# Padded constants, units pinned to source order, and wider openings in the gated merges of a hybrid decoder layer

## The chip, the cores and the metric

The kernel runs on one core of one Trainium2 chip. The metric is the device time in microseconds (us) of the whole program. The kernel before takes 2725.5 us (median of 3 runs, 2723.21 to 2727.9).

## What is computed

One decoder layer over 512 tokens of 2048 channels, in fp32. A modulated norm of x gives u; one wide input projection of u feeds three token mixers (A: differential attention, B: retention, C: dilated windows), their SiLU gates and three merge gates; the gated branches are merged and go through w_out.

```python
u = rms_norm(x, norm_w) * (1.0 + scale[:, None]) + shift[:, None]
proj = jnp.einsum('bsd,de->bse', u, w_in)
...
y_a = jnp.einsum('bsw,wd->bsd', o_a.astype(dt) * jax.nn.silu(a_z), w_proj_a)
y_b = jnp.einsum('bsw,wd->bsd', o_b.astype(dt) * jax.nn.silu(b_z), w_proj_b)
y_c = jnp.einsum('bsw,wd->bsd', o_c.astype(dt) * jax.nn.silu(c_z), w_proj_c)
merged = jax.nn.sigmoid(g_a) * y_a + jax.nn.sigmoid(g_b) * y_b + jax.nn.sigmoid(g_c) * y_c
y = jnp.einsum('bsd,de->bse', merged, w_out)
return x + gate[:, None] * y
```

## The kernel before, in words

**Precision.** Every operand of a matmul is kept as a high part (fp32r) and a low part (the rest). A product is three matmuls (`mm3`, L148 to L151): high by high, high by low, low by high. So each weight tile is loaded by SP, cast by ACT (the high part) and subtracted by DVE (the low part), in `w_half` (L144, L145), for the units in `pure_prep` (L549, L550) and `sum_prep` (L580 to L582).

**Stages**, in us from the start of the span:

- 0 to 244: modulation, norm, u, and the first merge-gate columns, as high and low products of u by weights.
- 244 to 974, the units: nine "units" of 1024 columns of w_in (five for values, four for merge gates of A and B) are made by a Strassen-like scheme with seven products instead of eight. A unit is 14 jobs. Six are plain (P1, P2, R3, two jobs each): load 1 MB, cast, low part, matmuls. Eight are sum jobs (j = 0 to 7): load, four sums in place (L580), cast (L581), low part (L582), matmuls into four results R6, R5, R7 and Q4. A job of a value unit is 24 matmuls of 512 columns, one of a gate unit (`fm=True`) 48 of 256. In a value unit the tokens are the stationary operand, in a gate unit the weights. The loop at L652 prepares job i + 1, then multiplies job i; in the first eight jobs `form_build` also makes the sums of tokens (the forms). When a group of products is complete its `done` runs: `keep`, `p2_done` or `sum_done`, with DVE sums, a sigmoid on ACT for gate units, and a write on POOL's queue.
- 974 to 1678, eight C heads; 1776 to 2092, eight A heads; 2212 to 2432, four pairs of B heads. Each is a row of projections (`proj`, two halves of 1024 rows, 48 matmuls of 512) with the attention work of the head put between the halves as `mid`.
- 1678 to 1776, 2092 to 2212 and 2432 to 2537, a gate phase after each (`gate_phase`, L692): 16 blocks db of 128 columns, 24 matmuls each; the result times the merge gate (L730), plus the part so far (L729 loads it into gpr, L732 adds), written back to part.
- 2537 to 2722: the product with w_out, residual and final norm.

**Memory.** Pools lie on the left or the right side of SBUF. The constants come first on the left; weights for the stages after the units, xr, xh and xl of the units, and mh and ml lie on the left; u (uh, ul), the forms (fh, fl) and the mixers' results (yh, yl) on the right. The weights of the first stage are on the right as well. `xr` has three buffers, `xh` and `xl` two each. PSUM has two tiles `pj` and six tiles `at`.

**What sets the order.** The framework schedules the instructions into one queue per engine, which then runs in order. It may put an instruction ahead of one that stands earlier in the source if it expects it to be ready sooner; source order is the priority. `tc.keep_in_program_order(ins)` ties `ins` behind the instruction that was traced before it on the same engine; it orders issue only and waits for nothing else. No instruction of the units is tied before the change.

**Gate phases.** `y_start` opens a block's product with six of eight slots of y, in an `at` tile, because the last two slots come late. Three blocks are opened ahead (`ahead`), with the leftovers of the last head (`left`) run between them; then each block is closed with j = 6 and 7.

**Bias of the C gates.** `gate_bias_load` (L671) loads and sums on POOL into br (one buffer), `gate_bias_sum` closes it with one matmul (L688). `bias_step` runs at each C head and a second time in head 1.

Of the kernel before, what the change touches and what calls it, by code (L numbers as in the profile page):

```python
# [17 lines left out]
P = 128  # L18
# [46 lines left out]
def hybrid_kernel(ctx, tc, x, c, w_in, w_pa, w_pb, w_pc, w_out, w_ada, b_ada, norm_w, lam,  # L65
# [49 lines left out]
    nlam = const.tile([P, 1], F32, tag="nlam", name="nlam")  # L115
    daw = const.tile([P, 1], F32, tag="daw", name="daw")

    uh = [up.tile([P, S], F32R, tag=f"uh{i}", name=f"uh{i}") for i in range(KC)]
    ul = [up.tile([P, S], F32R, tag=f"ul{i}", name=f"ul{i}") for i in range(KC)]

# [12 lines left out]
    def w_half(src, k0, c0, rot=False, tiles=None, low=dve):  # L133
# [11 lines left out]
            low.tensor_sub(l, r, h.bitcast(F32))  # L145
        return h, l

    def mm3(ps, ah, al, bh, bl, start, stop):  # L148
        nc.tensor.matmul(ps, lhsT=ah, rhs=bh, start=start, stop=False)  # L149
        nc.tensor.matmul(ps, lhsT=ah, rhs=bl, start=False, stop=False)  # L150
        nc.tensor.matmul(ps, lhsT=al, rhs=bh, start=False, stop=stop)  # L151
# [12 lines left out]

    def perm(ap):
# [335 lines left out]
    def form_build(j):  # L501

        if j % 2 == 0:
            r = wxp.tile([P, 4, 512], F32, tag="xr", name="xr", bufs=3)
            for i in range(2):
                nc.sync.dma_start(out=r[:, 2 * i:2 * i + 2, :],
                                  in_=u_dram[i * HJ + j:i * HJ + j + 2].rearrange("j p t -> p j t"))
            form_rows[0] = r
        r, jj = form_rows[0], j % 2
        d = evp.tile([P, 4, 256], F32, tag=("z", "s")[jj], name="d")  # L510
        a11, a21 = r[:, jj, 0:256], r[:, jj, 256:512]
        a12, a22 = r[:, 2 + jj, 0:256], r[:, 2 + jj, 256:512]
        dve.tensor_sub(d[:, 0, :], a21, a22)
        dve.tensor_sub(d[:, 1, :], a11, d[:, 0, :])
        dve.tensor_sub(d[:, 3, :], a21, a11)
        dve.tensor_sub(d[:, 2, :], a12, d[:, 1, :])
        act.copy(fh[j], d)
        dve.tensor_sub(fl[j], d, fh[j].bitcast(F32))

    def tokens(name, j, qs):  # L520

# [19 lines left out]
    def unit_jobs(w, c0, put, fm=False, early=False):  # L541
# [17 lines left out]
        def keep(key, tag):  # L559
            t = evp.tile([P, 2, 512], F32, tag=tag, name=tag)  # L560
            for q in range(2):
                act.copy(t[:, q, :], st[key][q])
            st[tag] = t

        def p2_done():
            t = evp.tile([P, 2, 512], F32, tag="c", name="c")
            for q in range(2):
                dve.tensor_add(t[:, q, :], st["p1"][:, q, :], st["P2"][q])
            put(t, 0, 0)
            if early:  # L570
                nc.gpsimd.dma_start(out=p1_dram, in_=st["p1"])

        def sum_prep(j):
            r, h, l = x_tiles()
            for i in range(2):
                nc.sync.dma_start(out=r[:, 2 * i:2 * i + 2, :],
                                  in_=w[(i * HJ + j) * P:(i * HJ + j + 1) * P, c0:c0 + 1024]
                                  .rearrange("p (a c) -> p a c", a=2))
            for o, a in ((0, 1), (1, 3), (3, 0), (2, 3)):
                dve.tensor_add(r[:, o, :], r[:, o, :], r[:, a, :])  # L580
            act.copy(h, r)  # L581
            dve.tensor_sub(l, r, h.bitcast(F32))  # L582
            return h, l

        def sum_mul(j, hl):
# [10 lines left out]
        def sum_done():  # L596
            z = evp.tile([P, 2, 512], F32, tag="z", name="z")
            s = evp.tile([P, 2, 512], F32, tag="s", name="s")
            r3, p1 = st["r3"], st["p1"]
            for q in range(2):  # L600
                dve.tensor_sub(z[:, q, :], st["R6"][q], p1[:, q, :])
            for q in range(2):
                dve.tensor_add(s[:, q, :], z[:, q, :], st["R5"][q])
            dve.tensor_add(r3, r3, s)
            put(r3, 0, 512)
            for q in range(2):
                dve.tensor_add(z[:, q, :], z[:, q, :], st["R7"][q])
                dve.tensor_add(s[:, q, :], s[:, q, :], st["R7"][q])
            put(s, 1, 512)
            for q in range(2):  # L610
                dve.tensor_sub(z[:, q, :], st["Q4"][q], z[:, q, :])
            put(z, 1, 0)

        lists = []
        for key, name, k0, cc, done in (("P1", "A11", 0, 0, lambda: keep("P1", "p1")),
                                        ("P2", "A12", 1024, 0, p2_done),
                                        ("R3", "2", 1024, 512, lambda: keep("R3", "r3"))):
            lists.append([(lambda k0=k0, cc=cc, t=t: pure_prep(k0 + t * 512, c0 + cc),
                           lambda hl, key=key, name=name, t=t: pure_mul(key, name, t, hl),
                           done if t == HJ // 4 - 1 else None) for t in range(HJ // 4)])  # L620
        lists.append([(lambda j=j: sum_prep(j), lambda hl, j=j: sum_mul(j, hl),
                       sum_done if j == HJ - 1 else None) for j in range(HJ)])
        return lists[0] + lists[1], lists[2] + lists[3]

    def put_values(unit):
# [21 lines left out]
    for n, b in enumerate([NF - 1] + list(range(NF - 1))):  # L647
        if n % 2 == 0:
            t = evp.tile([P, 2, 512], F32, tag=("p1", "c", "r3", "s")[n // 2], name="raw")
        (act.copy if n % 2 == 0 else dve.tensor_copy)(t[:, n % 2, :], ps[b])  # L650
        nc.scalar.dma_start(out=graw_dram[NF + NM + b], in_=t[:, n % 2, :])
    for i, (_, mul, done) in enumerate(jobs):  # L652
        nxt = jobs[i + 1][0]() if i + 1 < len(jobs) else None
        if i < HJ:
            form_build(i)
        mul(ready)
        ready = nxt
        if done is not None:
            done()
    wx_es.close()  # L660
    ev_es.close()
    fo_es.close()
# [23 lines left out]
    def gate_bias_sum(db, br):  # L686
        pc = at()
        nc.tensor.matmul(pc[:, 0:1], lhsT=br, rhs=ones[:, 0:1], start=True, stop=True)  # L688
# [250 lines left out]
    for hd in range(8):  # L939
# [187 lines left out]
    for pr in range(4):  # L1127
# [25 lines left out]
        szs = [silu(bp, proj(B_Z + (2 * pr + a) * P, mid=lambda a=a, rest=rest: rest(a)), tag=f"sz{a}", bufs=1)  # L1153
               for a in range(2)]

        def values(a, pr=pr, vpair=vpair, pts=pts, got=got):
# [126 lines left out]
```

## Time and profile before

| what | us |
|---|---|
| median of 3 runs | 2725.5 |
| the profiled execution | 2723.54 |
| its span | 2721.8 |
| first stage, 0 to 120 and 120 to 244: PE busy | 95.76 and 115.24 |
| C heads, 974 to 1678: PE busy of 704 | 693.01 |
| gate phase C, 1678 to 1776: PE busy of 98 | 95.35 |
| A heads, 1776 to 2092: PE busy of 316 | 314.31 |
| w_out, 2537 to 2722: PE busy of 185 | 176.51 |

The profile is of one execution. The engines are PE (matmuls), DVE (vector), ACT (scalar), POOL and SP (which issues most loads). In a group of instructions, a line reads: code line, engine, operation, output and inputs with shapes, count, then busy time and mean ns of one, then idle time of the engine just before them and what ended it. In a timeline, a row is start, duration, engine, line, and in brackets the idle time before it. A matmul's duration in the records overlaps the next one's, so the pace of PE is read from start to start. A line of the waits is: who waited, for whom, then us in total, number of waits, the longest.

### The profile page before, as it was taken

What the parts mean: (1) busy time and instruction counts of PE and PEld (TensorE: products, weight loads), DVE (VectorE), ACT (ScalarE), POOL (GpSimd) and SP (SyncE); (2) the same over time, 40 slices, a digit from 0 to 9 for tenths busy, and PEclk for the clock granted to TensorE, in tenths of its full rate; (3) what the DMA queues carried; (4) which work ended last, traced back from release to release, by engine and by line L of the source; (5) the groups of instructions that cost most, each with busy time, mean ns of one, the idle gap of its engine ahead of it and who ended that gap; (6) DMA issues with size and microseconds to landing.
All of it is one profiled execution on the core that took longest, in us unless ns stands there. A gap on an engine that the chain in (4) does not pass through costs nothing.

```text
span 2721.8 us, 33257 instructions
## 1 busy us (share of the span) xinstructions
PE 2608.9 (96%) x13091; PEld 2184.7 (80%) x13091; DVE 1698.1 (62%) x2455; ACT 1034.2 (38%) x1388; POOL 265.2 (10%) x271
## 2 busy tenths in 40 slices
PE   6899999999999999899999999999999899998998
PEld 5777777778999978688888888788887677777888
DVE  7985887777787744344443444657666667776434
ACT  4224433334343433333333333246665124443222
POOL 3331000000000022222211220000000000000000
PEclk9999999999999999999999999999999899999999
DMA  9777666666666654344443444942322672325632
GB/s 347 246 268 253 221 213 209 216 216 203 208 199 205 209 134 137 89 117 114 115 117 103 112 122 116 285 133 79 92 86 86 222 246 87 107 82 171 217 103 101
DMA packets 413420, 448.17 MB, mean 165 GB/s; under 512 B 24696, under 2 KB 308042, under 8 KB 412112
## 3 DMA queue, kind: packets, MB, share of 16 engines
q1 hardware_dynamic: 383784, 395.61, 46.0%
q0 software_dynamic: 9760, 33.59, 4.0%
q10 hardware_dynamic: 19720, 16.86, 1.8%
q8 instruction: 102, 1.67, 0.3%
q14 instruction: 54, 0.44, 0.1%
HBM read 405.56 MB, written 40.44 MB: 164 GB/s over the span
## 4 chain that ended last, share of the span: by engine, by line
PE 77%; DVE 12%; DMA 6%; ACT 2%; issue 2%; POOL 0%; SPq 0%; ACTq 0%; DVEq 0%; POOLq 0%
PE pj L151 15%; PE pj L149 14%; PE pj L150 14%; PE at L150 10%; PE at L151 10%; PE at L149 10%; DVE acc L309 3%; DMA xr<-in_w_in_dram 2%; DVE xl L550 1%; DMA part<-gsg 1%; DVE rs L992 1%; DVE rt L1102 1%; DVE wl L145 1%; ACT xh L549 1%; DMA gpr<-part 1%
## 5 line engine op out<-in xcount | busy, mean ns | idle before, releaser
L151 PE MATMUL pj<-uh,wl 128*128 128x512 f32 x1552 | 616.6, 397 | 11.2 <-DVE wl L145 8.7
L149 PE MATMUL pj<-uh,wh 128*128 128x512 f32 x1552 | 620.5, 400 | 4.8 <-ACT wh L144 4.8
L150 PE MATMUL pj<-ul,wh 128*128 128x512 f32 x1552 | 614.8, 396 | 0.0
L145 DVE TENSOR_TENSOR wl<-wr,wh 128x1024 fp32r<-128x1024 f32 x226 | 285.2, 1263 | 383.1 <-ACT wh L144 363.8
L144 ACT CAST wh<-wr 128x1024 fp32r<-128x1024 f32 x228 | 238.8, 1049 | 562.7 <-PE pj L150 411.3
L151 PEld LDWEIGHTS pj<-uh,wl 128*128 128x128 f32 x1552 | 293.5, 189 | 83.0 <-DVE wl L145 11.2
L149 PEld LDWEIGHTS pj<-uh,wh 128*128 128x128 f32 x1552 | 293.7, 189 | 69.8 <-ACT wh L144 5.0
L150 PEld LDWEIGHTS pj<-ul,wh 128*128 128x128 f32 x1552 | 294.0, 189 | 65.9
L581 ACT CAST xh<-xr 128x2048 fp32r<-128x2048 f32 x72 | 137.6, 1912 | 238.6 <-PE at L150 89.1
L580 DVE TENSOR_TENSOR xr<-xr 128x512 f32<-128x512 f32 x288 | 197.1, 689 | 42.7 <-DMA xr<-in_w_in_dram 36.9
L582 DVE TENSOR_TENSOR xl<-xr,xh 128x2048 fp32r<-128x2048 f32 x72 | 164.8, 2290 | 46.3 <-ACT xh L581 46.2
L149 PE MATMUL at<-yh,wh 128*128 128x512 f32 x384 | 156.5, 408 | 18.3 <-ACT yh L215 11.7
L151 PE MATMUL at<-yh,wl 128*128 128x512 f32 x384 | 155.5, 405 | 4.9 <-DVE wl L145 4.9
L550 DVE TENSOR_TENSOR xl<-xr,xh 128x2048 fp32r<-128x2048 f32 x54 | 123.7, 2291 | 54.3 <-ACT xh L549 54.1
L150 PE MATMUL at<-yl,wh 128*128 128x512 f32 x384 | 155.4, 405 | 0.0
L549 ACT CAST xh<-xr 128x2048 fp32r<-128x2048 f32 x54 | 103.0, 1910 | 128.4 <-PE at L150 51.0
L150 PE MATMUL at<-fl,xh 128*128 128x256 f32 x384 | 108.1, 281 | 0.0
L149 PE MATMUL at<-fh,xh 128*128 128x256 f32 x384 | 108.1, 281 | 0.0
L151 PE MATMUL at<-fh,xl 128*128 128x256 f32 x384 | 108.1, 281 | 0.0
L149 PEld LDWEIGHTS at<-yh,wh 128*128 128x128 f32 x384 | 74.5, 194 | 38.0 <-ACT yh L215 12.9
L150 PE MATMUL at<-xl,fh 128*128 128x512 f32 x240 | 94.8, 395 | 0.8 <-DVE xl L550 0.8
L151 PE MATMUL at<-xh,fl 128*128 128x512 f32 x240 | 94.7, 395 | 0.0
(407 smaller groups left out, 5130.1 us busy)
## 6 DMA issues: line engine op xcount, KB each, us to landing
wr<-in_w_in_dram SPq DMA_DIRECT2D x196, 512.0 KB, 3.8
xr<-in_w_in_dram SPq DMA_DIRECT2D x144, 512.0 KB, 4.4
xr<-in_w_in_dram SPq DMA_DIRECT2D x54, 1024.0 KB, 5.7
wa<-in_w_ada_dram SPq DMA_DIRECT2D x20, 1024.0 KB, 10.3
gwa<-in_w_ada_dram SPq DMA_DIRECT2D x32, 512.0 KB, 5.8
wr<-in_w_out_dram SPq DMA_DIRECT2D x32, 512.0 KB, 4.0
wr<-in_w_in_dram SPq DMA_DIRECT2D x32, 448.0 KB, 6.6
wb<-in_w_ada_dram SPq DMA_DIRECT2D x12, 1024.0 KB, 8.7
```

The source lines that it names most:

```text
L144: act.copy(h, r)
L145: low.tensor_sub(l, r, h.bitcast(F32))
L149: nc.tensor.matmul(ps, lhsT=ah, rhs=bh, start=start, stop=False)
L150: nc.tensor.matmul(ps, lhsT=ah, rhs=bl, start=False, stop=False)
L151: nc.tensor.matmul(ps, lhsT=al, rhs=bh, start=False, stop=stop)
L309: dve.scalar_tensor_tensor(out=acc, in0=wa[:, j, :], scalar=sc[:, k:k + 1], in1=acc, op0=ALU.mult, op1=ALU.add)
L549: act.copy(h, r)
L550: dve.tensor_sub(l, r, h.bitcast(F32))
L580: dve.tensor_add(r[:, o, :], r[:, o, :], r[:, a, :])
L581: act.copy(h, r)
L582: dve.tensor_sub(l, r, h.bitcast(F32))
L992: dve.reciprocal(rs, rs)
```

## The change

1. A constant `pad` of 32 fp32 values per partition is added behind the other constants.
2. In the loop over the units, and only there, `pin` calls `keep_in_program_order` on the matmuls and on the vector and scalar work of the preparations, `form_build` and the finishes. `sum_done` is cut into three parts; the last job's parts run one per job (all that are left when a group with a single part is done).
3. `proj` asks for the weights of its second half before `mid()` and not after it.
4. `br` gets two buffers, and the extra bias load is made in head 4 and not in head 1; all open sums are closed at each step.
5. In a gate phase, six blocks are opened with seven of eight slots (`mode == "last"`: four blocks with six slots), the first two in `pj` tiles; the leftovers come every second opening (every opening in the last phase). The missing slots of all opened blocks come from one wide load `h7`, `l7`. In the last pair of B, the first of the leftovers moves into the last projection's `mid`.

```diff
+    pad = const.tile([P, 32], F32, tag="pad", name="pad")
+    dve.memset(pad, 0.0)
...
+    pinned = [False]
+
+    def pin(instr):
+
+        if pinned[0]:
+            tc.keep_in_program_order(instr)
...
-        nc.tensor.matmul(ps, lhsT=ah, rhs=bh, start=start, stop=False)
...
+        pin(nc.tensor.matmul(ps, lhsT=ah, rhs=bh, start=start, stop=False))
...
         ps = pj()
+        nxt = w_half(w_in, 0, c0, rot, tiles[0])
         for half in range(2):
-            h, l = w_half(w_in, half * 1024, c0, rot, tiles[half])
+            h, l = nxt
             for j in range(8):
                 k = half * 8 + j
                 mm3(ps, h[:, j, :], l[:, j, :], uh[k], ul[k], k == 0, k == KC - 1)
-            if half == 0 and mid is not None:
-                mid()
+            if half == 0:
+                nxt = w_half(w_in, 1024, c0, rot, tiles[1])
+                if mid is not None:
+                    mid()
...
             for o, a in ((0, 1), (1, 3), (3, 0), (2, 3)):
-                dve.tensor_add(r[:, o, :], r[:, o, :], r[:, a, :])
-            act.copy(h, r)
-            dve.tensor_sub(l, r, h.bitcast(F32))
+                pin(dve.tensor_add(r[:, o, :], r[:, o, :], r[:, a, :]))
+            pin(act.copy(h, r))
+            pin(dve.tensor_sub(l, r, h.bitcast(F32)))
             return h, l
...
+        def done_z():
+            z = st["z"] = evp.tile([P, 2, 512], F32, tag="z", name="z")
             for q in range(2):
-                dve.tensor_sub(z[:, q, :], st["R6"][q], p1[:, q, :])
+                pin(dve.tensor_sub(z[:, q, :], st["R6"][q], st["p1"][:, q, :]))
+
+        def done_s():
+            z, r3 = st["z"], st["r3"]
+            s = st["s"] = evp.tile([P, 2, 512], F32, tag="s", name="s")
             for q in range(2):
-                dve.tensor_add(s[:, q, :], z[:, q, :], st["R5"][q])
-            dve.tensor_add(r3, r3, s)
+                pin(dve.tensor_add(s[:, q, :], z[:, q, :], st["R5"][q]))
+            pin(dve.tensor_add(r3, r3, s))
             put(r3, 0, 512)
+
+        def done_rest():
+            z, s = st["z"], st["s"]
...
+    pinned[0] = True
+    later = []
     for i, (_, mul, done) in enumerate(jobs):
         nxt = jobs[i + 1][0]() if i + 1 < len(jobs) else None
         if i < HJ:
             form_build(i)
         mul(ready)
         ready = nxt
-        if done is not None:
-            done()
+        later += done
+        for _ in range(len(later) if len(done) == 1 else min(1, len(later))):
+            later.pop(0)()
+    pinned[0] = False
+    for f in later:
+        f()
...
-        br = pool.tile([P, P], F32, tag="br", name="br", bufs=1)
+        br = pool.tile([P, P], F32, tag="br", name="br", bufs=2)
...
+        n_ahead, late = (4, 2) if mode == "last" else (6, 1)
...
-        def y_start(db):
+        def y_start(db, nj):
             h, l = w_half(w_p[0], 0, db * P)
-            py = at()
-            for j in range(6):
-                mm3(py, h[:, j, :], l[:, j, :], yh[j], yl[j], j == 0, False)
-            return py, h, l
+            py = pj() if db < 2 else at()
+            for j in range(nj):
+                mm3(py, h[:, j, :], l[:, j, :], yh[j], yl[j], j == 0, j == 7)
+            return py
...
-        for db in range(3):
-            ahead[db] = y_start(db)
-            if left:
+
+        for db in range(n_ahead):
+            ahead[db] = y_start(db, 8 - late)
+            if left and db % (3 - late) == 0:
                 left.pop(0)()
+        r, h7, l7 = w_tiles([P, late, n_ahead * P])
+        nc.sync.dma_start(out=r, in_=w_p[0, 1024 - late * P:1024, 0:n_ahead * P].rearrange("(j p) c -> p j c", p=P))
+        act.copy(h7, r)
+        dve.tensor_sub(l7, r, h7.bitcast(F32))
...
-            py, h, l = ahead.pop(db) if db in ahead else y_start(db)
+            if db < n_ahead:
+                py = ahead.pop(db)
+                cs = slice(db * P, (db + 1) * P)
+                for j in range(late):
+                    y = 8 - late + j
+                    mm3(py, h7[:, j, cs], l7[:, j, cs], yh[y], yl[y], False, y == 7)
+            else:
+                py = y_start(db, 8)
             sg = sgs.pop(db)
-            for j in (6, 7):
-                mm3(py, h[:, j, :], l[:, j, :], yh[j], yl[j], False, j == 7)
...
     def bias_step():
-        if bias_open:
-            gate_bias_sum(*bias_open.pop())
+        while bias_open:
+            gate_bias_sum(*bias_open.pop(0))
+        bias_more()
+
+    def bias_more():
...
-        if hd == 1:
-            bias_step()
+        if hd == 4:
+            bias_more()
...
+        def z_mid(a, rest=rest, pr=pr, vpair=vpair, pts=pts, got=got):
+            rest(a)
+            if pr == 3 and a == 1:
+                b_values(2 * pr, *vpair, pts[0], got[0])
...
-    gate_phase(G_B, w_pb, "last", mh, ml, left=left, then=merged_open)
+    gate_phase(G_B, w_pb, "last", mh, ml, left=left[1:], then=merged_open)
```

More of the change, by code (lines that the diff above doesn't have):

```diff
@@ L146, in w_half @@
         return h, l
+    pinned = [False]
+    def pin(instr):
+        if pinned[0]:
+            tc.keep_in_program_order(instr)
     def mm3(ps, ah, al, bh, bl, start, stop):
-        nc.tensor.matmul(ps, lhsT=ah, rhs=bh, start=start, stop=False)
-        nc.tensor.matmul(ps, lhsT=ah, rhs=bl, start=False, stop=False)
-        nc.tensor.matmul(ps, lhsT=al, rhs=bh, start=False, stop=stop)
+        pin(nc.tensor.matmul(ps, lhsT=ah, rhs=bh, start=start, stop=False))
+        pin(nc.tensor.matmul(ps, lhsT=ah, rhs=bl, start=False, stop=False))
+        pin(nc.tensor.matmul(ps, lhsT=al, rhs=bh, start=False, stop=stop))
     def proj(c0, rot=False, tiles=(None, None), mid=None):
         ps = pj()
+        nxt = w_half(w_in, 0, c0, rot, tiles[0])
         for half in range(2):
-            h, l = w_half(w_in, half * 1024, c0, rot, tiles[half])
+            h, l = nxt
             for j in range(8):
@@ L512, in form_build @@
         a12, a22 = r[:, 2 + jj, 0:256], r[:, 2 + jj, 256:512]
[L513 to L518, printed above, removed]
+        pin(dve.tensor_sub(d[:, 0, :], a21, a22))
+        pin(dve.tensor_sub(d[:, 1, :], a11, d[:, 0, :]))
+        pin(dve.tensor_sub(d[:, 3, :], a21, a11))
+        pin(dve.tensor_sub(d[:, 2, :], a12, d[:, 1, :]))
+        pin(act.copy(fh[j], d))
+        pin(dve.tensor_sub(fl[j], d, fh[j].bitcast(F32)))
     def tokens(name, j, qs):
@@ L561, in keep @@
             for q in range(2):
-                act.copy(t[:, q, :], st[key][q])
+                pin(act.copy(t[:, q, :], st[key][q]))
             st[tag] = t
@@ L567, in p2_done @@
             for q in range(2):
-                dve.tensor_add(t[:, q, :], st["p1"][:, q, :], st["P2"][q])
+                pin(dve.tensor_add(t[:, q, :], st["p1"][:, q, :], st["P2"][q]))
             put(t, 0, 0)
@@ L579, in sum_prep @@
             for o, a in ((0, 1), (1, 3), (3, 0), (2, 3)):
-                dve.tensor_add(r[:, o, :], r[:, o, :], r[:, a, :])
-            act.copy(h, r)
-            dve.tensor_sub(l, r, h.bitcast(F32))
+                pin(dve.tensor_add(r[:, o, :], r[:, o, :], r[:, a, :]))
+            pin(act.copy(h, r))
+            pin(dve.tensor_sub(l, r, h.bitcast(F32)))
             return h, l
@@ L594, in sum_mul @@
                 block_mul(st[key], name, j, hl[0][:, o, :], hl[1][:, o, :], fm)
[L596 to L599, printed above, removed]
+        def done_z():
+            z = st["z"] = evp.tile([P, 2, 512], F32, tag="z", name="z")
             for q in range(2):
-                dve.tensor_sub(z[:, q, :], st["R6"][q], p1[:, q, :])
+                pin(dve.tensor_sub(z[:, q, :], st["R6"][q], st["p1"][:, q, :]))
+        def done_s():
+            z, r3 = st["z"], st["r3"]
+            s = st["s"] = evp.tile([P, 2, 512], F32, tag="s", name="s")
             for q in range(2):
-                dve.tensor_add(s[:, q, :], z[:, q, :], st["R5"][q])
-            dve.tensor_add(r3, r3, s)
+                pin(dve.tensor_add(s[:, q, :], z[:, q, :], st["R5"][q]))
+            pin(dve.tensor_add(r3, r3, s))
             put(r3, 0, 512)
+        def done_rest():
+            z, s = st["z"], st["s"]
             for q in range(2):
-                dve.tensor_add(z[:, q, :], z[:, q, :], st["R7"][q])
-                dve.tensor_add(s[:, q, :], s[:, q, :], st["R7"][q])
+                pin(dve.tensor_add(z[:, q, :], z[:, q, :], st["R7"][q]))
+                pin(dve.tensor_add(s[:, q, :], s[:, q, :], st["R7"][q]))
             put(s, 1, 512)
             for q in range(2):
-                dve.tensor_sub(z[:, q, :], st["Q4"][q], z[:, q, :])
+                pin(dve.tensor_sub(z[:, q, :], st["Q4"][q], z[:, q, :]))
             put(z, 1, 0)
@@ L619, in unit_jobs @@
                            lambda hl, key=key, name=name, t=t: pure_mul(key, name, t, hl),
-                           done if t == HJ // 4 - 1 else None) for t in range(HJ // 4)])
+                           (done,) if t == HJ // 4 - 1 else ()) for t in range(HJ // 4)])
         lists.append([(lambda j=j: sum_prep(j), lambda hl, j=j: sum_mul(j, hl),
-                       sum_done if j == HJ - 1 else None) for j in range(HJ)])
+                       (done_z, done_s, done_rest) if j == HJ - 1 else ()) for j in range(HJ)])
         return lists[0] + lists[1], lists[2] + lists[3]
@@ L1151, in rest @@
             b_scores(2 * pr + a, ks_[a], qs[a], pts[a])
-        szs = [silu(bp, proj(B_Z + (2 * pr + a) * P, mid=lambda a=a, rest=rest: rest(a)), tag=f"sz{a}", bufs=1)
+        def z_mid(a, rest=rest, pr=pr, vpair=vpair, pts=pts, got=got):
+            rest(a)
+            if pr == 3 and a == 1:
+                b_values(2 * pr, *vpair, pts[0], got[0])
+        szs = [silu(bp, proj(B_Z + (2 * pr + a) * P, mid=lambda a=a, z_mid=z_mid: z_mid(a)), tag=f"sz{a}", bufs=1)
                for a in range(2)]
```

## The prediction

> **What bounds the kernel now.** I read the page's busy times first, then the groups, then the stretches, then what PE waited for, and last the rows of the stretch that the change rewrites most.
>
> ```profile
> PE 2608.9 (96%) x13091; PEld 2184.7 (80%) x13091; DVE 1698.1 (62%) x2455; ACT 1034.2 (38%) x1388; POOL 265.2 (10%) x271
> ...
> L151 PE MATMUL pj<-uh,wl 128*128 128x512 f32 x1552 | 616.6, 397 | 11.2 <-DVE wl L145 8.7
> ...
> L581 ACT CAST xh<-xr 128x2048 fp32r<-128x2048 f32 x72 | 137.6, 1912 | 238.6 <-PE at L150 89.1
> L580 DVE TENSOR_TENSOR xr<-xr 128x512 f32<-128x512 f32 x288 | 197.1, 689 | 42.7 <-DMA xr<-in_w_in_dram 36.9
> L582 DVE TENSOR_TENSOR xl<-xr,xh 128x2048 fp32r<-128x2048 f32 x72 | 164.8, 2290 | 46.3 <-ACT xh L581 46.2
> L149 PE MATMUL at<-yh,wh 128*128 128x512 f32 x384 | 156.5, 408 | 18.3 <-ACT yh L215 11.7
> ```
>
> PE is the bound: 2608.9 of 2721.8 us. So only two things shorten this kernel: fewer PE idle times (113 us in all), or a shorter step from one matmul to the next. The 1552 and 384 are the counts of one of three lines each (L149 to L151). The three groups L580, L581, L582 are the preparation of a "sum" job in the units stage: four sums, a cast, a low part. The stretches (start and end, length, PE busy, and so on; granted clock near the end):
>
> ```profile
> core 0: us, PE busy (x) PEld busy (x) DVE busy (x) ACT busy (x) POOL busy (x), PEclk, DMA share, GB/s
> ...
> 244.00:974.00 730.00, 709.04 (x4345) 630.25 (x4343) 565.01 (x565) 281.03 (x185) 26.87 (x37) 1.00 0.62 209
> ...
> 2092.00:2212.00 120.00, 102.64 (x412) 80.56 (x411) 76.25 (x114) 30.78 (x46) 0.00 (x0) 0.91 0.70 223
> 2212.00:2432.00 220.00, 209.80 (x914) 168.03 (x913) 168.30 (x264) 99.53 (x178) 0.00 (x0) 0.98 0.37 109
> 2432.00:2537.00 105.00, 97.24 (x413) 77.56 (x412) 62.36 (x74) 33.73 (x43) 0.00 (x0) 0.95 0.52 156
> ```
>
> The units stage (244 to 974) is PE-bound: 21.0 us idle of 730. Gate phase A (2092 to 2212) idles 17.4 us, the B pairs (2212 to 2432) 10.2, gate phase B (2432 to 2537) 7.8. In the waits of PE:
>
> ```profile
> PE at L149 <- ACT yh L215: 11.7, 3, 6.4
> PE at L688 <- POOL br L683: 10.2, 1, 10.2
> PE pj L151 <- DVE wl L145: 8.7, 6, 1.9
> ```
>
> **Part 1, units in source order.** The pins make the queues of PE, and of DVE and ACT for this loop's own work, follow the source. Source order on DVE is: four sums of job j+1, low part of j+1, four sums of j+2, and so on; and each low part waits for ACT's cast of the same job, which waits for its sums. Before, DVE does not run like that:
>
> ```profile
> 766.64 2.14 DVE L580 TENSOR_TENSOR xr<-xr 128x512 f32<-128x512 f32 x3 [0.30 <-DMA xr<-in_w_in_dram]
> 769.71 0.69 DVE L580 TENSOR_TENSOR xr<-xr 128x512 f32<-128x512 f32 x1 [0.93 <-DMA xr<-in_w_in_dram]
> 770.32 2.28 DVE L582 TENSOR_TENSOR xl<-xr,xh 128x2048 fp32r<-128x2048 f32 x1
> 772.52 2.14 DVE L580 TENSOR_TENSOR xr<-xr 128x512 f32<-128x512 f32 x3
> 774.87 2.29 DVE L582 TENSOR_TENSOR xl<-xr,xh 128x2048 fp32r<-128x2048 f32 x1 [0.20 <-ACT xh L581]
> 777.08 2.86 DVE L580 TENSOR_TENSOR xr<-xr 128x512 f32<-128x512 f32 x4
> ```
>
> ```profile
> 772.92 1.91 ACT L581 CAST xh<-xr 128x2048 fp32r<-128x2048 f32 x1 [3.78 <-PE at L150]
> ```
>
> The three sums at 772.52 run while ACT casts (772.92 to 774.83) the tile whose low part starts at 774.87: they belong to the next job, and fill the wait for the cast. In source order they can't. What remains is a loop with nothing beside it: four sums 2.86 (the x4 row), 0.04 to the cast, cast 1.91, 0.04 to the low part (774.87 − 774.83; I take the same for the other hand-over), and 2.20 until DVE takes its next operation (772.52 − 770.32): **7.05 us per sum job**.
>
> What PE needs for one sum job comes from its steps:
>
> ```profile
> 700.19 0.28 PE L149 MATMUL at<-uh,xh 128*128 128x256 f32 x1
> ...
> 701.97 0.28 PE L149 MATMUL pj<-fh,xh 128*128 128x256 f32 x1
> ...
> 1298.61 0.40 PE L150 MATMUL pj<-ul,wh 128*128 128x512 f32 x1
> ...
> 1301.64 0.39 PE L151 MATMUL pj<-uh,wl 128*128 128x512 f32 x1
> ...
> 2598.79 0.39 PE L151 MATMUL at<-wh,ml 128*128 128x512 f32 x1
> ...
> 2601.74 0.39 PE L149 MATMUL at<-wh,mh 128*128 128x512 f32 x1
> ```
>
> The gate units make 48 matmuls of 256 a job, 15 steps in 1.78 us, 118.7 ns: 5.70 us. The value units make 24 of 512, 13 steps in 3.03 us, 233.1 ns: 5.59, or 5.45 at the 226.9 ns of the last pair (13 steps in 2.95), which the pad may give (part 2). So the loop is 1.60 us too slow for PE in value units and 1.35 in gate units. A plain job needs only 1.91 + 0.04 + 2.20 = 4.15, so it gives a lead of 1.3 to 1.55, and no more, since xh and xl have two buffers. It hides the first sum job of a value unit; the other seven show: 5 units × 7 × 1.60 = 56. In gate units the sums of the finish use that lead: 4 × 8 × 1.35 = 43. Added at the boundaries: in order, the sigmoids of a gate unit's finish stand on ACT ahead of the next casts, and the finish's ten or so DVE operations ahead of the next low part. Followed through the three queues with the durations above, that is about 4.6 us at each of three boundaries (14), and 5 where the second unit's sums follow the first's finish after only two plain jobs. Sum 118. It takes off what idles at unit boundaries now, about 11 of the 21.0 (the rest is the start's loads and the wait at the end, both kept), and 3 for faster plain jobs. The first eight jobs also build the forms, in order now behind loads from u_dram: the trace has no such order; between −2 and +12 us, I take +3. Together +107.
>
> Bounds: were the four sums spaced as far as the lone one (770.32 − 769.71 = 0.61), the loop is 6.63 and the same sum gives 35 × 1.18 + 32 × 0.93 + 19 − 11 − 3 + 3 = +79. And the boundary terms, followed in the queues and in no row, may be nothing: +60. High end +118 with the forms at +12. Since three terms are at their worst in +107, I take **+95**. Behind the waiting low part stand the next job's sums, and PE waits for all of it.
>
> **Part 2, the pad.** 128 bytes behind the constants move every tile on the left. Before, tiles on the left start 128 bytes apart from those on the right, modulo 512; with the pad they agree. In w_out both operands lie on the left: 226.9 ns a step. In the projections the weights are on the left and u on the right: 233.1. If the offset is the cause, 6.2 ns go from 1552 × 3 projection and 384 × 3 gate-phase matmuls: 4656 × 6.2 = 28.9 and 1152 × 6.2 = 7.1, 36.0 in all; less 2 that I leave for what falls on waits, **−34**, with nothing to hide it, since PE is the bound there. At 256 wide nothing is taken (118.7 ns now). Bounds: 0 and −45. The Trainium skill, SBUF — State Buffer, section "Who interferes with whom", gives TensorE two independent read ports and says that "PE and ACT never wait on anyone". By that rule addresses would not matter and this term would be 0; the rows' 226.9 against 233.1 do not agree with it so far, but other things differ between those stages too.
>
> **Part 3, bias tiles.** br gets two buffers and the fifth head, not the second, takes the extra load; a sum on PE then follows loads a whole head old. The 10.2 us of L688 go: **−10**; POOL has time, its 265.2 us lie in 2721.8. Kept end: 0, if the wait moves to the fifth head.
>
> **Part 4, projections.** The second half's weights (their DMA on SP, cast on ACT, low part on DVE) are asked for ahead of mid(), so they pass mid()'s loads and vector work. That meets the six waits for wl (8.7 us); I take **−5**: mid()'s own work comes up to a low part later. Bounds −9 and +3.
>
> **Part 5, gate phases.** B: the last pair's first values move up and four products are opened over six slots; the 6.4 us wait for yh goes: **−6** (bounds −8 and 0). A and C: six products opened over seven parts each cover the waits for the last yh, and one wide load replaces three small ones. But each of the 16 blocks of A goes through one gpr buffer: load, add, write. The first and the last of its 16 adds:
>
> ```profile
> 2125.04 0.68 DVE L732 TENSOR_TENSOR gsg<-gsg,gpr 128x512 f32<-128x512 f32 x1
> ...
> 2218.75 0.67 DVE L732 TENSOR_TENSOR gsg<-gsg,gpr 128x512 f32<-128x512 f32 x1
> ```
>
> That is 6.25 us a block, more than PE's 24 × 0.233 = 5.59. Opening more delays the first block's end by about what it saves, and the chain then ends the phase. Between −17 (all of A's idle time) and +7 (half of three more openings of 21 × 0.233 = 4.9 us each); I take **−4** for A and C together.
>
> **The sum** on the profiled run (2723.5 us: 2721.8 and 1.7 around it): 2723.5 + 95 − 34 − 10 − 5 − 6 − 4 = 2759.5. The median of the three runs is 2.0 above that run. Forecast **2760**; about 0.2%, 5.5 us, is what a measurement of this kernel can tell from no change.
>
> **The rivals.** First, faster: DVE's chain does not bind. It decides at a loop of 5.6 us: if the sums still run during the cast, or are much shorter when alone, PE stays the bound in the units. Then part 1 is −11 for the boundaries, +3 for the forms, and the pad's 6.2 ns on all 5 × 14 × 24 matmuls of the value units, −10: −18. Total 2723.5 − 18 − 34 − 10 − 5 − 6 − 4 = 2646.5. For it: DVE's own work is 4 × 0.689 + 2.29 = 5.05 a job, less than PE's. Against it: one queue in order can't take j+2's sums while it waits for j+1's low part. Chance 0.18.
>
> Second, the pad does nothing, as in the rule above: the 6.2 ns come from which tiles or stages they are. 2759.5 + 34 + 3 = 2796. For it: the first reason is only a match of addresses. Chance 0.15.
>
> Third, the loop is real but its size nearer to the low end, and the gate phases and projections give all they can: 2723.5 + 60 − 38 − 10 − 9 − 8 − 17 = 2701.5. For it: each bound is from a row. Against it: all must go one way. Chance 0.12.
>
> The forecast's own case has 0.55: with part 1 from +79 to +118 and the rest as taken, 2743 to 2783.
>
> **How the numbers follow.** Faster: the first rival, 0.18, and most of the third, 0.10: 0.28. The same: 0.04. Slower: 0.68. The range takes in the pad rival at the top with a little for the forms, 2800, and at the bottom the third rival and the upper edge of the first (where the gate phases give nothing), 2660.
>
> **What would show it.** In the DVE rows after: four sums, a gap of 1.9 us that ends on the cast, a low part, four sums, with 7.05 from one to the next; PE idle about 1.6 (value) or 1.35 (gate) in each sum job, waiting for xl of L582, some 90 us in all; the units stage some 95 longer. Steps of 227 ns in the projections, a C head, with its seven projections of 48, 336 × 6.2 ns = 2.1 us shorter. No wait at the bias sum. If low parts still alternate with sums of the next job, part 1 is wrong and the kernel is faster; if the steps stay at 233, part 2 is.

## The result, and the profile after

The changed kernel takes 2812.01 us (median of 4 runs, 2811.04 to 2813.63) against 2726.7 for the kernel before: a ratio of 1.0316, 95% interval 1.0298 to 1.0333. It is slower, as forecast, but by 85 us where 34 were forecast, and above the range's upper end of 2800.

The page of the changed kernel, busy times and the three groups of a sum job (L593 to L595 are what L580 to L582 were):

```profile
PE 2604.4 (93%) x13091; PEld 2192.3 (78%) x13091; DVE 1707.8 (61%) x2459; ACT 1036.0 (37%) x1391; POOL 267.3 (10%) x271
...
L594 ACT CAST xh<-xr 128x2048 fp32r<-128x2048 f32 x72 | 137.4, 1908 | 368.5 <-DVE xr L593 337.1
L595 DVE TENSOR_TENSOR xl<-xr,xh 128x2048 fp32r<-128x2048 f32 x72 | 165.1, 2292 | 153.0 <-ACT xh L594 153.0
L593 DVE TENSOR_TENSOR xr<-xr 128x512 f32<-128x512 f32 x288 | 198.9, 691 | 7.4
```

The work is the same; what is new is who waits. The cast now waits 337.1 us for the sums and the low part 153.0 us for the cast (46.2 before), 2.1 us in each of 72 jobs. The longest waits of PE:

```profile
PE pj L160 <- DVE xl L595: 50.6, 38, 1.7
PE pj L161 <- DVE xl L595: 36.6, 32, 1.2
PE pj L161 <- DVE wl L148: 10.5, 8, 1.9
PE at L159 <- ACT wh L147: 9.0, 1, 9.0
```

The first two rows are 70 waits for the low parts of sum jobs, 87.2 us in all. In the units of the kernel before, PE has 6 such waits, 5.1 us:

```profile
PE pj L151 <- DVE xl L582: 3.2, 4, 1.7
PE pj L150 <- DVE xl L582: 1.9, 2, 1.4
```

Cut at the first matmul of each stage, the stretches compare so (the predicted column spreads the terms of the sum, the pad by its 6.2 ns and the counts of matmuls; its 2 us for waits are left out):

| stretch | before | after | change | predicted |
|---|---|---|---|---|
| start | 238.3 | 239.8 | +1.5 | 0 |
| units | 736.5 | 863.8 | +127.3 | +95 |
| C heads | 703.3 | 677.0 | −26.3 | −26.7 |
| gate phase C | 98.3 | 101.3 | +3.0 | −4.4 |
| A heads | 316.3 | 311.6 | −4.7 | −7.1 |
| gate phase A | 120.1 | 111.4 | −8.7 | −4.4 |
| B pairs | 219.7 | 226.7 | +7.0 | −9.8 |
| gate phase B | 104.6 | 96.7 | −7.9 | −8.4 |
| w_out and end | 184.7 | 183.6 | −1.1 | 0 |

Of the 90 us between the two profiled spans (2811.9 less 2721.8), the units are 127 and everything else together −37, where −61 was expected by this table. Outside the units, the B pairs (+7.0 for −9.8) and gate phase C (+3.0 for −4.4) miss most. These stretches are of one profile each: among runs whose code is the same in a gate phase or in the B pairs, one such stretch differs by up to 4.4 us. The same stretches of the changed kernel in the view of stretches, for PE's share and its granted clock:

```profile
239.80:1103.60 863.80, 743.15 (x4369) 647.69 (x4368) 578.24 (x573) 284.86 (x191) 27.56 (x38) 0.98 0.53 180
...
2193.50:2304.90 111.40, 96.26 (x412) 76.84 (x411) 74.62 (x111) 30.91 (x46) 0.00 (x0) 0.94 0.73 228
2304.90:2531.60 226.70, 210.62 (x924) 170.54 (x923) 171.80 (x270) 101.90 (x182) 0.00 (x0) 0.97 0.39 115
```

The timeline of DVE, and then of ACT, inside the sum jobs of a value unit:

```profile
584.59 2.29 DVE L595 TENSOR_TENSOR xl<-xr,xh 128x2048 fp32r<-128x2048 f32 x1 [2.10 <-ACT xh L594]
586.79 2.87 DVE L593 TENSOR_TENSOR xr<-xr 128x512 f32<-128x512 f32 x4
591.76 2.29 DVE L595 TENSOR_TENSOR xl<-xr,xh 128x2048 fp32r<-128x2048 f32 x1 [2.10 <-ACT xh L594]
```

```profile
589.81 1.91 ACT L594 CAST xh<-xr 128x2048 fp32r<-128x2048 f32 x1 [5.26 <-DVE xr L593]
```

It is the loop that was forecast: low part, four sums, an idle wait that ends on the cast, low part. It takes 591.76 − 584.59 = 7.17 us, not 7.05: the hand-over from the sums (end 589.66) to the cast (589.81) is 0.15 and not 0.04. PE, in the same job:

```profile
585.15 0.39 PE L159 MATMUL pj<-xh,fh 128*128 128x512 f32 x1
586.93 0.50 PE L160 MATMUL pj<-xl,fh 128*128 128x512 f32 x1 [1.40 <-DVE xl L595]
587.27 0.39 PE L161 MATMUL pj<-xh,fl 128*128 128x512 f32 x1
587.50 0.40 PE L159 MATMUL pj<-xh,fh 128*128 128x512 f32 x1
```

The first product runs, the second needs the low part and starts 1.78 us after it, where a step is 0.23. Note the step behind the stall as well: 0.34 us from 586.93 to 587.27.

### The profile page after: what moved, and what is told of

Its sections match the earlier page's. It is cut to its first block, busy times and chain, and to the rows that moved or that the text cites. A ratio compares the mean times of both kernels' runs of the same rounds, so it can differ in the third digit from the quotient of the medians.

```text
span 2811.9 us, 33272 instructions
## 1 busy us (share of the span) xinstructions
PE 2604.4 (93%) x13091; PEld 2192.3 (78%) x13091; DVE 1707.8 (61%) x2459; ACT 1036.0 (37%) x1391; POOL 267.3 (10%) x271
## 3 DMA queue, kind: packets, MB, share of 16 engines
q8 instruction: 102, 1.67, 0.2%
## 4 chain that ended last, share of the span: by engine, by line
PE 49%; DVE 5%; DMA 5%; issue 2%; ACT 2%; SPq 0%; ACTq 0%; DVEq 0%
PE pj L159 12%; PE pj L161 12%; PE pj L160 12%; PE at L160 4%; PE at L159 4%; PE at L161 4%; DMA part<-gsg 2%; DMA gpr<-part 1%; DVE rt L1142 1%; DVE xr L593 1%; DMA gsg<-graw 1%; ACT xh L594 1%; DVE wl L148 1%; DVE rs L1032 0%; PE at L1049 0%
## 5 line engine op out<-in xcount | busy, mean ns | idle before, releaser
L161 PE MATMUL pj<-uh,wl 128*128 128x512 f32 x1552 | 610.1, 393 | 13.1 <-DVE wl L148 10.5
L159 PE MATMUL pj<-uh,wh 128*128 128x512 f32 x1552 | 613.6, 395 | 5.8 <-ACT wh L147 4.8
L160 PE MATMUL pj<-ul,wh 128*128 128x512 f32 x1552 | 608.0, 392 | 0.0
L594 ACT CAST xh<-xr 128x2048 fp32r<-128x2048 f32 x72 | 137.4, 1908 | 368.5 <-DVE xr L593 337.1
L595 DVE TENSOR_TENSOR xl<-xr,xh 128x2048 fp32r<-128x2048 f32 x72 | 165.1, 2292 | 153.0 <-ACT xh L594 153.0
L593 DVE TENSOR_TENSOR xr<-xr 128x512 f32<-128x512 f32 x288 | 198.9, 691 | 7.4
L159 PE MATMUL at<-yh,wh 128*128 128x512 f32 x336 | 134.7, 401 | 12.3 <-ACT wh L147 9.0
L161 PE MATMUL at<-yh,wl 128*128 128x512 f32 x336 | 133.7, 399 | 0.9 <-DVE wl L148 0.8
L160 PE MATMUL at<-yl,wh 128*128 128x512 f32 x336 | 133.5, 397 | 0.0
L159 PE MATMUL at<-xh,fh 128*128 128x512 f32 x240 | 94.7, 395 | 5.0 <-DVE s L619 5.0
```

What stands on the lines that cost most here:

```text
L159: pin(nc.tensor.matmul(ps, lhsT=ah, rhs=bh, start=start, stop=False))
L160: pin(nc.tensor.matmul(ps, lhsT=ah, rhs=bl, start=False, stop=False))
L161: pin(nc.tensor.matmul(ps, lhsT=al, rhs=bh, start=False, stop=stop))
L593: pin(dve.tensor_add(r[:, o, :], r[:, o, :], r[:, a, :]))
L594: pin(act.copy(h, r))
L595: pin(dve.tensor_sub(l, r, h.bitcast(F32)))
```

## The experiments

Stretches below are cut at the first matmul of a stage in the profile of each run. All ratios are to the kernel before, which took 2722.7 to 2725.8 beside the various runs.

**Without the pins.** Theory: DVE's source order is the loss. Rival: the finish in three parts or another edit is.

```diff
-    pinned[0] = True
```

> The changed kernel with no instruction pinned; all else as in it. If the pins are what costs (DVE's loop of 7.17 us per sum job), the units stage falls from 863.8 us to about 725 and the time from 2812 to about 2675 to 2690. If the finish in three parts or the other edits cost, it stays above 2750.

Measured 2676.58, ratio 0.9818 (0.9804 to 0.9833). The units take 725.9 us, 10.6 less than before the change:

```profile
238.80:964.70 725.90, 708.50 (x4370) 638.63 (x4368) 566.91 (x571) 283.57 (x190) 27.58 (x38) 1.00 0.62 213
```

Against the changed kernel this is 135 us less; the units alone are 137.9 shorter. The pins turn a gain of 1.8% into a loss of 3.2%.

**Pins kept, the sums one job earlier.** Theory: only the sums' place in the queue costs. Rival: any fixed order of the queues costs.

```diff
-        nxt = jobs[i + 1][0]() if i + 1 < len(jobs) else None
+        nxt = x_cast(rows[i + 1]) if i + 1 < len(jobs) else None
+        if i + 2 < len(jobs):
+            rows.append(jobs[i + 2][0]())
+        if nxt is not None:
+            x_low(rows[i + 1], nxt)
```

Here the first function of a job only loads and, in a sum job, makes the four sums; x_cast and x_low are the pinned cast and low part.

> The changed kernel with all its pins, but the load and the four sums of a sum job stand one job earlier in the source, between the cast and the low part of the job before. If the loss is the sums' place in DVE's queue, a sum job takes PE's 5.45 to 5.76 us again, the units stage about 725, the time 2675 to 2695. If holding PE, ACT and DVE to any one order is what costs, it stays above 2760.

Measured 2717.59, ratio 0.9968 (0.9957 to 0.9978): neither 2675 to 2695 nor above 2760. DVE and ACT in the sum jobs:

```profile
618.75 2.87 DVE L601 TENSOR_TENSOR xr<-xr 128x512 f32<-128x512 f32 x4
621.55 2.29 DVE L520 TENSOR_TENSOR xl<-xr,xh 128x2048 fp32r<-128x2048 f32 x1
623.76 2.86 DVE L601 TENSOR_TENSOR xr<-xr 128x512 f32<-128x512 f32 x4
626.99 2.29 DVE L520 TENSOR_TENSOR xl<-xr,xh 128x2048 fp32r<-128x2048 f32 x1 [0.37 <-ACT xh L516]
```

```profile
619.60 1.92 ACT L516 CAST xh<-xr 128x2048 fp32r<-128x2048 f32 x1 [3.09 <-PE at L161]
625.04 1.92 ACT L516 CAST xh<-xr 128x2048 fp32r<-128x2048 f32 x1 [3.52 <-PE at L161]
```

The sums run under the cast, and the job takes 5.44 us (cast to cast), PE's 24 × 0.227; the cast waits for PE again. So in the sum jobs the theory holds: the same queues, as strictly in order, lose nothing once the sums stand there. But the units still take 766.4, 40.5 more than without pins. By the count of PE's steps that the next section explains, 22.7 of these are longer stalls and 17.5 are slower matmuls behind them. The stalls come from the rest of the order: PE waits of up to 2.7 us for low parts in the first eight jobs, where the forms are built, one wait of 5.8 us for a finish, and two waits (1.66 and 1.82 us) at each of the three boundaries of gate units.

**Pins on PE and ACT only.**

```diff
-        if pinned[0]:
+        if pinned[0] and instr.ins.engine != mybir.EngineType.DVE:
```

> The changed kernel with the pins on TensorE and ScalarE only, VectorE free. If DVE's order alone makes the loop of 7.17 us, sum jobs go at PE's pace, and only the sigmoids at the three boundaries of gate units still hold back the casts: units about 726 + 3 x 5 = 741, time about 2692. If the order on PE or ACT is what costs, above 2760.

Measured 2680.19, ratio 0.9836 (0.9819 to 0.9853); units 730.5:

```profile
239.80:970.30 730.50, 713.81 (x4370) 641.88 (x4369) 570.56 (x572) 285.28 (x191) 27.68 (x38) 0.99 0.63 213
```

All but 4.6 us of the 137.9 in the units hangs on VectorE's order; no run pins VectorE alone. The boundaries cost less than expected (730.5, not 741): with DVE free, the stalls there are one step of 2.4 us and three of 0.7 to 0.9.

**The pad alone, on the kernel before.**

```diff
+    pad = const.tile([P, 32], F32, tag="pad", name="pad")
+    dve.memset(pad, 0.0)
```

> The kernel before with the 128 bytes of constants alone. If the step of a matmul of 512 hangs on the two operands' addresses, it falls from 232 to 227 ns in projections, gate phases and value units: 2726 less 34 to 45, about 2680 to 2692. If the place does not matter, 2726.

Measured 2695.57, ratio 0.9886 (0.9872 to 0.9901). The wait at the bias sum is still there, so the pad does not touch it:

```profile
PE at L691 <- POOL br L686: 10.4, 1, 10.4
```

**The changed kernel without the pad.** The same two lines taken out.

> The changed kernel without the pad. If the pad is worth 6 ns on each matmul of 512 in projections and gate phases, 2812 + 33 = 2845, and nothing in the sum jobs of the units, which DVE's loop of 7.17 us sets. If the pad is worth nothing, 2812.

Measured 2841.2, ratio 1.0422 (1.0407 to 1.0438): 29.2 us above the changed kernel, of which 2.6 in the units (866.4 against 863.8). With 30.2 for the pad alone both ways agree.

**The pad with 64 and with 256 bytes, on the kernel before.** Theory: the distance between the places of the two operands, modulo 512, sets the step (the time from one matmul's start to the next one's). Rival: any shift helps.

```diff
-    pad = const.tile([P, 32], F32, tag="pad", name="pad")
+    pad = const.tile([P, 16], F32, tag="pad", name="pad")
```

and with 64 in the place of 16.

> The kernel before with a pad of 64 bytes: tiles on the left stand 64 bytes off those on the right, modulo 512, where before it was 128. If the step follows the distance, it lies between 227 and 233 ns, time about 2710; if only equal places help, 2726; if any shift of the constants helps, 2695.

> The kernel before with a pad of 256 bytes: 128 bytes off on the other side. If the distance between the two operands, modulo 512, sets the step, it is 232 to 233 ns again and the time 2726. If a later start of the left tiles is what helps, 2695 or less.

64 bytes: 2709.91, ratio 0.9945 (0.993 to 0.996). 256 bytes: 2725.5, ratio 1.0 (0.9988 to 1.0012). A distance of 0 gives 2695.6, 64 gives 2709.9, 128 on either side 2725: the rival is out. That the distance counts modulo 512 is not shown: a period of 256 would give the same four times. The step of the projections in the changed kernel (distance 0), then with 64 bytes:

```profile
1249.78 0.39 PE L161 MATMUL pj<-uh,wl 128*128 128x512 f32 x1
...
1253.86 0.39 PE L161 MATMUL pj<-uh,wl 128*128 128x512 f32 x1
```

```profile
1309.66 0.39 PE L153 MATMUL pj<-ul,wh 128*128 128x512 f32 x1
...
1313.79 0.39 PE L153 MATMUL pj<-ul,wh 128*128 128x512 f32 x1
```

18 steps take 4.08 us (226.7 ns) and 4.13 us (229.4 ns), against 233.1 in the prediction's row. In a value unit, 64 bytes gain nothing:

```profile
561.49 0.39 PE L152 MATMUL pj<-xh,fh 128*128 128x512 f32 x1
...
565.69 0.39 PE L152 MATMUL at<-xh,uh 128*128 128x512 f32 x1
```

These 18 steps take 4.20 us (233.3 ns); with the full pad alone, 18 steps of a value unit take 4.08 (560.09 to 564.17 in its trace). In the projections the weights, on the left, are the stationary operand; in a value unit the tokens, on the right, are. So the same 64 bytes count one way round and not the other, and the distance alone does not say it all. In w_out, where both operands lie on one side, the mean of the steps below 0.26 us is 226.7 to 226.8 ns in the kernel before and with each of the three pads.

**No pins, and the projections as before.** `w_half` of the second half behind mid() again.

> The changed kernel with no pins, and the second half's weights of a projection asked for behind mid() as before. If the earlier request does nothing (the waits of about 2.1 and 1.6 us in each pair of B heads are still there in the changed kernel), 2677 as without the pins alone, within 3. If it hides waits elsewhere, 2681 to 2686.

Measured 2671.82, ratio 0.9807 (0.9793 to 0.982): not slower, and by the medians 4.8 us faster than without pins alone, though the intervals of the ratios overlap. The waits of PE for wl in the B pairs are 9.7 us in 7 here and 9.9 in 7 with the early request; it removed none of them.

**No pins, and gate phases A and C as before.** The old `gate_phase` for these two, the new one for B.

> The changed kernel with no pins, and gate phases A and C opened as before (three blocks of six slots in at tiles); gate phase B stays new. If the load, add, write chain of gate phase A ends that phase and holds up the first B projections, A's own stretch grows by about 4 us, the B pairs shrink by about 8 and gate phase C by 2: 2671. If the wider openings save what PE waited for, 2690.

Measured 2670.29, ratio 0.9801 (0.9787 to 0.9815). Gate phase A takes 115.1 (112.3 with wide openings), the B pairs 223.0 (226.8), gate phase C 99.7 (100.1). As expected in sign and smaller in each, but no larger than such stretches differ between runs of the same code; the intervals of the ratios overlap.

**Both of these.**

> Both of the last two edits: no pins, gate phases A and C and the projections as before; what stays new is the pad, the finish in three parts, the bias tiles and gate phase B. If the two do not touch each other, 2671; if the earlier request pays for what the merges leave, 2680.

Measured 2667.48, ratio 0.9792 (0.9775 to 0.9809): the lowest median of this study, 2.1% below the kernel before; its interval overlaps those of all the other versions without pins. It keeps the pad, the finish in three parts, the bias tiles and the new gate phase B (96.2 us).

**The same with gate phase A new.**

> The changed kernel with no pins, projections and gate phase C as before, gate phases A and B new. Gate phase C 97 us as in the run with both old, A and the B pairs together about 337 either way: 2668, no different from the version with A as before too (2667.5).

Measured 2671.48, ratio 0.9799 (0.9777 to 0.982); no difference can be told, as expected.

**No pins, more buffers in gate phase A.**

```diff
-            sgs[db] = gp.tile([P, S], F32, tag="gsg", name="gsg", bufs=2)
+            if mode == "mid" and db > 1:
+                sgs[db] = gmp.tile([P, S], F32, tag="gsgm", name="gsg", bufs=4)
+            else:
+                sgs[db] = gp.tile([P, S], F32, tag="gsg", name="gsg", bufs=2)
```

and gpr with three buffers in the same way.

> The changed kernel with no pins, and in gate phase A alone gsg has four buffers (from the third block on) and gpr three, taken from the pool that opens there. If the chain through these buffers (load, add, write) is what ends the phase 19 us behind its matmuls and holds up the first B projections, the last add comes within 8 us of the last matmul, the B pairs fall from 226.8 to about 220 and the time from 2677 to about 2669. If the traffic of the phase or the order on SP sets it, no change: 2677.

Measured 2670.92, ratio 0.9802 (0.9788 to 0.9815). The last add now starts at 2178.29, 1 us behind the first matmul of the B pairs at 2177.3, the B pairs take 216.7 us (226.8), and PE's wait for k0h falls from 4.5 to 0.2. So the chain through these buffers is what held up the first B pair. But gate phase A itself takes 120.7 (112.3), so that A and the B pairs together fall only from 339.1 to 337.4, and the interval of the ratio overlaps that without pins alone. A's new longest wait, and the one for k0h:

```profile
PE at L159 <- ACT wh L147: 16.6, 1, 16.6
...
PE at L1158 <- ACT k0h L1186: 0.2, 1, 0.2
```

## Why the prediction was wrong, and where it was right

**The loop was right.** Its place (DVE's low part ahead of the next job's sums), its length (7.17 measured, 7.05 forecast) and its sign are shown by three runs: without pins, without DVE's pins, and with the sums moved. The stalls per sum job (mostly 1.56 to 1.60 us in value units and 1.31 to 1.32 in gate units) are those of the text. Counting each start-to-start distance over 0.4 us beyond a step, PE's stalls in the units rise from 24.8 to 134.7 us, by 109.9: the working had 118 − 11 + 3 = 110 for them. The terms inside miss a little, both ways: sum jobs of value units 54.9 (56 forecast), of gate units 41.7 (43), the three boundaries 11.4 (14), the place behind the first finish 9.3 (5). That these add up to 117.3 against 118 is partly luck, for they cancel.

**The step that failed is the choice of +95 out of that working.** I took the middle of bounds whose lower end (sums spaced by 0.61) no row supported for four sums in one chain, although the x4 row gave 2.86 for just that. The units took 127.3, 32 more than forecast; that is most of the 54 us by which the sum for the profiled run (+36) fell short of the 90 measured. Of the terms taken to be "at their worst", two came out worse still: the loop is longer by 0.12, and the first eight jobs, taken at +3, have eight stalls of 1.1 to 2.1 us. (The high end of +118 is a slip as well: by its own terms, 118 − 11 − 3 + 12, it is +116.)

**A term was missing: what a stall does to the matmuls behind it.** In the units 202 other steps are more than a fifth longer than the usual one, 24.2 us above it in all, where before there were 18 with 1.9 us. Nearly half of these (11.0 us) are mostly single steps behind a stall (0.34 for 0.23 us above). The rest (13.2 us) lie where the granted clock is 0.50; they come in runs, the longest at the boundaries of gate units:

```profile
821.39 0.38 PE L159 MATMUL at<-uh,xh 128*128 128x256 f32 x1 [1.67 <-ACT xh L562]
821.62 0.28 PE L160 MATMUL at<-ul,xh 128*128 128x256 f32 x1
823.72 0.58 PE L161 MATMUL at<-uh,xl 128*128 128x256 f32 x1 [1.82 <-DVE xl L563]
824.10 0.42 PE L159 MATMUL at<-uh,xh 128*128 128x256 f32 x1
...
829.01 0.41 PE L161 MATMUL at<-uh,xl 128*128 128x256 f32 x1
829.22 0.33 PE L159 MATMUL at<-uh,xh 128*128 128x256 f32 x1
829.39 0.28 PE L160 MATMUL at<-ul,xh 128*128 128x256 f32 x1
```

```profile
817.00:832.00 15.00, 11.50 (x73) 11.09 (x72) 5.69 (x5) 6.00 (x6) 1.50 (x2) 0.77 0.69 244
```

```profile
819.00:822.40 3.40, 1.22 (x9) 0.81 (x7) 1.03 (x1) 3.40 (x4) 0.63 (x1) 1.00 0.91 302
822.50:829.30 6.80, 5.58 (x26) 5.58 (x27) 3.37 (x2) 0.64 (x1) 0.00 (x0) 0.50 0.67 232
```

From 824.10 to 829.22 a step is 0.213 us and not 0.119: 24 steps in 5.12 us, some 2.3 us lost. The granted clock is 1.00 up to 822.4 and 0.50 from 822.5: it fell behind the idle time of 1.67 us and about 0.6 us into that of 1.82. Elsewhere in this trace a single idle time was enough:

```profile
389.94 0.39 PE L161 MATMUL at<-xh,ul 128*128 128x512 f32 x1
392.16 0.60 PE L159 MATMUL pj<-xh,fh 128*128 128x512 f32 x1 [1.84 <-ACT xh L594]
```

```profile
389.00:392.40 3.40, 1.56 (x7) 0.94 (x5) 1.36 (x3) 1.90 (x1) 0.00 (x0) 1.00 0.48 186
392.42:399.20 6.78, 5.06 (x12) 3.74 (x12) 4.69 (x5) 1.83 (x1) 0.00 (x0) 0.50 0.46 155
```

The Trainium skill, TensorE: Matmul & The Clock Gate, Part 1, section "What's actually happening", has the slow state follow an idle window of about 3.4 us; the idle times before these two drops are shorter, and the measurement decides. Length alone does not decide either: in the B pairs an idle time of 1.30 us (to 2460.00) is followed by steps of 0.43 us from 2461.17 on, while the lone stalls of the sum jobs (idle for 1.40 us in value units, 1.15 in gate units, some 7 us apart) do not lower the clock; it is 1.00 from 399.3 to 822.4, and in this window of gate jobs:

```profile
744.00:817.00 73.00, 63.71 (x515) 61.88 (x514) 50.56 (x50) 21.85 (x14) 0.75 (x1) 1.00 0.48 159
```

So the units' +127.3 is +109.9 of stalls, +22.3 of slower steps, and −4.9 of the rest, for which the pad's shorter 512-column steps account.

**The pad: mechanism right, size too large.** It is worth 30.2 us alone and 29.2 in the changed kernel, against 34 outside the units and 3 in them. Outside the units the pad alone gives 26.5 us (the units shrink from 736.5 to 732.8), over 5808 matmuls 4.6 ns each and not 6.2. The stretch from which I took the step was one of 13 steps; over the C heads the mean of the steps below 0.26 us falls by 5.7 ns (232.9 to 227.2). The rest of the miss seems to be gain that falls on waits, more than the 2 us that I left for it, in the B pairs above all: the pad alone shortens them by 1.3 us where 4.8 was counted. The rival (no effect) is out for these operands: the same instructions take 226.7, 229.4 and 233.1 ns at three distances. The Trainium skill, SBUF — State Buffer, section "Who interferes with whom", says that PE never waits on anyone; it speaks of engines that get in each other's way, and to take it as "addresses would not matter" was wrong here. Why the place of PE's own operands counts, no run here shows.

**Bias: right.** No wait at the bias sum is among the changed kernel's waits; C heads shrink by 26.3 us where 26.7 was the sum.

**The early request of the weights: wrong.** −5 was taken, and the waits for wl in the B pairs are still there (9.9 us in 7). That the low part stands behind other vector work, and not behind a late load or cast, is what the unchanged waits suggest; no run moved that vector work.

**Gate phases: B right (−7.9 for −8.4), A no gain, C wrong.** A's own stretch shrank by 8.7 us for −4.4, but only the profile of the kernel before has it at 120.1; with the same old opening, the three runs with a pad alone have 115.0 to 116.6. And A and the B pairs together take 338.1 us, against 339.8 before and 334.7 to 335.1 in those three runs. What part 5 said of the load, add, write chain, that it ends the phase, came true: A's last add comes after the first B projection, and the rotation of B stands behind it on DVE:

```profile
2323.67 0.69 DVE L769 TENSOR_TENSOR gsg<-gsg,gpr 128x512 f32<-128x512 f32 x1 [1.31 <-DMA gpr<-part]
2324.28 0.68 DVE L1139 TENSOR_TENSOR rf<-pj,cos 128x512 f32<-128x512 f32 x1
```

That is 19 us after the first matmul of the B pairs (2304.9), and PE waits 4.5 us for k0h and 1.0 for the rotation. The run with more buffers shows this cause: with the last add 1 us behind that matmul, the B pairs fell by 10 us, though A paid 8.4 of it back. The 9.0 us wait within A has another: writes to part are issued from ACT's queue, and one that waits holds the next weights' cast behind it.

```profile
2270.97 7.86 ACTq L771 DMA_DIRECT2D part<-gsg  x2
2278.95 1.04 ACT L147 CAST wh<-wr 128x1024 fp32r<-128x1024 f32 x1 [14.68 <-DMA gsg<-g]
```

This one is read from the trace and not tried. The +3.0 of gate phase C stays open: the seven profiles with its old form have 96.9 to 100.4 us, the seven with the new one 100.1 to 105.0, so it is likely real, but no run takes it apart.

## What to carry to other kernels

Holding a queue to source order is only as good as the source order: write down each engine's queue with its waits, and look for an operation that waits for another engine while independent work stands behind it. Where a scheduler has hoisted such work, a pin takes it back; move the work in the source first. And when rows give a chain's length, forecast that length: do not cut it because other terms might be smaller, and add what the stalls themselves cost, in the steps behind them.

## What the runs showed of the hardware

A 512-column fp32r matmul's pace depended on how its two operands' places differ: in total time 0 bytes 2695.6, 64 bytes 2709.9, 128 on either side 2725 us, with the same instructions. The 64 bytes gave 229.4 ns a step with the weights on the left as the stationary operand, and 233.3 with the two sides' roles swapped. And an idle time of 1.84 us was followed by a granted clock of 0.50 for 6.8 us (0.213 us for a 0.119 us step in another such stretch), while lone stalls of 1.40 us, 7 us apart, left it at 1.00.
